# Constants in two loads, one more group of seven products, and new order tables in a one-core transformer step

## The chip, the cores and the metric

The kernel runs on one core of one Trainium2 chip. The metric is the device time of one execution in microseconds (us). TensorE is PE in the profile, VectorE is DVE, ScalarE is ACT, GpSimd is POOL, and SyncE, whose queue issues most of the DMAs, is SP. PEld is PE's loading of the stationary operand.

## What is computed

One layer for two groups of 128 tokens of width 2048, the context and the latent tokens. Cut to what matters:

```python
sh1, sc1, g1, sh2, sc2, g2 = silu(cond) @ w_ada + b_ada
h = rms_norm(x) * (1 + sc1) + sh1
qa, ka, va, qb, kb, vb, ga, gb = split(h @ w_in)       # q and k with RMS norms, rotary for A's latent tokens
o_a, o_b = attention_A(...), attention_B(...)           # A with a sink logit per head, B with a position bias
x = x + g1 * ((sigmoid(ga) * (o_a @ w_br_a) + sigmoid(gb) * (o_b @ w_br_b)) @ w_out)
h2 = rms_norm(x) * (1 + sc2) + sh2
x = x + g2 * (relu(h2 @ w_up) ** 2 @ w_down)
```

Outputs are both token groups and the context's new keys and values. All is float32.

## The kernel before

**Steps.** Every float32 operand is split into a high part that PE takes in one pass and the rest, and a product is three matmuls: high by high, low by high, high by low. The weights come as 456 steps. A plain step is one tile of 128x1024 (512 KB): SP loads it (`raw`), ACT copies its high part (`wH`, L112), DVE subtracts (`wL`, L272), and PE runs 12 matmuls of 512 columns (two row blocks, two token groups, three products; L347 to L349, at the start L474 to L476). `run()` goes through the steps in order, and the order on every engine comes from tables written into the file, mostly one digit for a step: `RUN` (how many steps ahead SP loads), `LOOK` and `AHEAD` (how many steps ahead DVE and ACT split), `DOTS` and `DOTS2` (at which steps DVE computes columns of the modulation, L1685), `JOBS` (at which steps the parts of the eight attention jobs run), `LO_DMA`, `XL_DMA`, `YL_DMA`, `T_DMA` (which subtractions POOL makes by a DMA that adds to its target, L278 and L279, in DVE's place).

**Groups of seven.** The up projection after its first two column blocks is done in pieces 1 to 7. A piece has eight positions of two steps each. A plain position takes 24 matmuls. A position named in `FAST` is a group of seven: it multiplies a two by two arrangement of blocks with seven products in place of eight, 21 matmuls, and ACT and DVE form sums of weight blocks for it (`t`, `XL`, `YB`, `tL`, `uL`; L1506 to L1517).

**Tiles.** Almost everything lies in one pool of `GEN` = 53 tiles of 128x1024 float32. A load waits until a tile is free. Some sums of the down projection (`DS_AWAY`) and two gates (`AWAY`) are written to memory and read back.

**Transposes.** An attention job transposes its probabilities either on PE, where it is named in `TE` (`probs_T`, L970), or in three parts: ACT writes the 16-bit halves apart (`probs_part`), SP issues a DMA transpose (`flip`, L1062), ACT joins the halves (`join_full`).

**Constants.** `load_consts` (L754) runs at step `CONST_AT[0]` and puts nine loads on SP's queue: the rope table, three norm weights and the sink logits, each of these four repeated over 128 partitions, and four caches. `pair_load` (L356) loads the tiles `araw` that PE uses as they are, for the first columns of the modulation (L365).

**Small tiles.** `SM` hands out small tiles from a ring of 14. `SCRATCH` is the size given to the program as `dynamic_dma_scratch_size`, which POOL's DMAs use.

Of the kernel before, what the change touches and what calls it, by code (L numbers as in the profile page):

```python
# [10 lines left out]
F32 = mybir.dt.float32  # L11
# [11 lines left out]
NH = 8  # L23
# [13 lines left out]
H_AT = 38  # L37
DOTS1 = [20, 27, 30, 34, 34, 34, 38, 42]
# [21 lines left out]
DIRECT = (3,)  # L60
LO_DMA = {186: 8, 205: 8, 218: 9, 357: 6, 402: 6, 448: 7, 455: 3}

LOOK = "320000020500002000113432224544355446105343223385524450433655335345220455511216541254444406744443240165443463136211143544456397555524342453545433224531546677753453557412434789853455586466303567898461134235331776545653214545433434534422123768733734502102522243854523655760005645555536452367642004332333245620031043144643220323340312252125324443413423321411333333446345833326123111223423654523544524557100124130023323212212653354124352222546524348984222137443"
RUN = "477775843203332344201115467652232043011000214655554545722223554564663425725104564635357113386532341025420431232200023641333255531301123352668485623663533674577742537976553665798745455424674845166864765894635788555673686472111145366178975888700000020012023644555422226413232347643568846245786634444454264413110226663556601331223412454545453312421521553234211233853234713364676798730111441302144857734435120022454125889556545654254345899778887778568999996432"
AHEAD = "431002222111211211100000000220000000000210121111110000000000011011122211000020133110000100000233000000011111112211133011020000023000000000000222001110010000000000000000111000222000100010221244331221020000000000011111000003022411110111110002000002111145220110000133444663455741000000000010001102100100000000000000000000000120000000000000112000211111223321000000000000000000000020000000000100000000011112223422222122100002120011100212112222234643010221345422"
CONST_AT = [73, 75]
XL_DMA = {9: 8, 16: 10, 21: 7, 23: 9, 26: 7, 35: 9, 38: 11, 43: 9, 55: 10, 61: 8}
ADA_G = ((1,), (2,), (3, 4), (5, 6))
ADA_AT = [None, 5, 14, 16, 22, 34, 40]
XS_AT = {1: 5, 2: 12, 3: 36}  # L70
POST = {('kvA', 0): [66, 70, 73], ('qA', 0): [66, 69, 75, 75, 77], ('qA', 1): [70, 75, 75, 82, 82], ('kB', 0): [75, 77, 79, 80, 82], ('qB', 0): [81, 82, 86, 88, 90], ('kB', 1): [84, 86, 91, 92, 95], ('qB', 1): [85, 92, 99, 100, 100]}
JOBS = [[80, 80, 81, 85, 88, 89, 92], [82, 83, 84, 86, 90, 97, 104], [83, 86, 86, 89, 90, 90, 105], [89, 91, 92, 93, 93, 105, 109], [95, 95, 98, 100, 100, 102, 114], [95, 101, 102, 104, 107, 111, 116], [106, 106, 108, 108, 121, 123, 127], [108, 111, 116, 117, 117, 120, 124]]
SS_G = [(0, 2), (2, 1)]
SS_AT = [53, 53, 73, 73, 125, 141]
T_AT = [3, 4]
PREP_IN = [4, 7]
DOTS = [37, 45, 46, 50, 50, 51, 52, 54, 56, 56, 56, 57, 61, 63, 65, 67, 70, 73, 77, 84, 89, 91, 92, 93, 96, 97, 102, 103, 104, 106, 108, 109, 109, 112, 114, 117, 118, 120, 122, 122, 123, 126, 129, 129, 129, 132, 133, 137, 138, 138, 140, 144, 145, 146, 156, 156, 156, 160, 160, 163, 167, 169, 173, 173, 175, 175, 178, 179, 179, 182, 182, 183]
DOTS2 = [225, 231, 234, 235, 237, 238, 245, 245, 258, 266, 268, 270, 270, 294, 300, 301, 306, 327, 328, 331, 333, 336, 349, 359, 360, 362, 363, 367, 394, 395, 396, 401]
# [12 lines left out]
def tile_hybrid_step(ctx: ExitStack, tc: tile.TileContext, a):  # L91
# [4 lines left out]
    sp = ctx.enter_context(tc.tile_pool(name="small", bufs=6))  # L96
# [3 lines left out]
    act, dve, pe, pool, sync = nc.scalar, nc.vector, nc.tensor, nc.gpsimd, nc.sync  # L100
# [37 lines left out]
    early = G("early")  # L138
# [615 lines left out]
    def load_consts():  # L754
        rope, wbg = G("rope"), cpadG[:, 640:1024]
        rc = rope[:, 0:256].rearrange("p (a b c) -> p a b c", a=2, b=4)
        sync.dma_start(rc.rearrange("p a b c -> p (a b c)"), a["rope"])
        wb = wbg.rearrange("p (a d) -> p a d", a=3)
        for n, name in enumerate(("q_norm_a", "k_norm_a", "k_norm_b")):
            sync.dma_start(wb[:, n, :], a[name][0].partition_broadcast(P))  # L760
        dve.tensor_scalar(wb, wb, float(HD) ** 0.5, None, op0=OP.mult)
        dve.tensor_scalar(qkw, qkw, float(HD) ** 0.5, None, op0=OP.mult)
        K2["wb"] = {"kvA": wb[:, 1, :], "kB": wb[:, 2, :]}

        for n, name in enumerate(("qA", "kvA")):
            t = rope[:, 256 * n + 256:256 * n + 512].rearrange("p (a b c) -> p a b c", a=2, b=4)
# [359 lines left out]
    for u in AWAY:  # L1126
        i = end_of(("y" + u[0][1].lower(), u[1]))
# [732 lines left out]
```

## Time and profile before

| what | before |
|---|---|
| median of 3 runs | 1313.22 us (1312.78 to 1313.6) |
| the profiled execution | 1312.65 us |
| its span, first to last instruction | 1310.8 us |
| PE busy in the span | 1303.2 us, 99% |
| DVE / ACT / POOL busy | 1126.5 / 904.5 / 57.4 us |
| mean granted clock of PE | 0.999 |

The profiled execution took 1.85 us more than its span; that lies outside the first and the last instruction. Busy PE includes the modelled ends of pipelined matmuls, so the pace is read from one start to the next.

### The profile page before, as it was taken

What the parts mean: (1) busy time and instruction counts of PE and PEld (TensorE: products, weight loads), DVE (VectorE), ACT (ScalarE), POOL (GpSimd) and SP (SyncE); (2) the same over time, 40 slices, a digit from 0 to 9 for tenths busy, and PEclk for the clock granted to TensorE, in tenths of its full rate; (3) what the DMA queues carried; (4) which work ended last, traced back from release to release, by engine and by line L of the source; (5) the groups of instructions that cost most, each with busy time, mean ns of one, the idle gap of its engine ahead of it and who ended that gap; (6) DMA issues with size and microseconds to landing.
All of it is one profiled execution on the core that took longest, in us unless ns stands there. A gap on an engine that the chain in (4) does not pass through costs nothing.

```text
span 1310.8 us, 17957 instructions
## 1 busy us (share of the span) xinstructions
PE 1303.2 (99%) x6333; PEld 1057.9 (81%) x6334; DVE 1126.5 (86%) x1446; ACT 904.5 (69%) x1145; POOL 57.4 (4%) x66
## 2 busy tenths in 40 slices
PE   9999999999999999999999999999999999999998
PEld 4778788788788878888888888888888888888887
DVE  4669799989999899999778998987999998789663
ACT  5635566699865655636786878859779597696980
POOL 0000000332000000000000000000000000000000
PEclk9999999999999999999999999999999999999999
DMA  9999999897999989997599789779977978869593
GB/s 371 408 409 408 400 409 389 346 321 232 271 347 349 386 294 365 359 334 235 205 300 318 204 269 287 275 269 273 322 240 238 362 245 278 301 205 367 193 355 96
DMA packets 170138, 400.90 MB, mean 306 GB/s; under 512 B 71840, under 2 KB 73088, under 8 KB 170048
## 3 DMA queue, kind: packets, MB, share of 16 engines
q1 hardware_dynamic: 165744, 387.36, 82.3%
q0 software_dynamic: 4160, 12.32, 5.0%
q8 instruction: 49, 0.80, 0.2%
q14 instruction: 41, 0.34, 0.1%
q10 hardware_dynamic: 144, 0.08, 0.1%
HBM read 373.97 MB, written 10.80 MB: 294 GB/s over the span
## 4 chain that ended last, share of the span: by engine, by line
PE 98%; ACT 1%; DMA 1%; SPq 0%; issue 0%; DVE 0%; ACTq 0%
PE acc L347 17%; PE acc L348 17%; PE acc L349 17%; PE Q L1421 6%; PE Q L1420 6%; PE Q L1419 6%; PE acc L474 5%; PE acc L475 5%; PE acc L476 5%; PE ps_ada L365 3%; PE ps_S L920 1%; PE Z L1421 1%; PE Z L1420 1%; PE Z L1419 1%; DMA araw<-in_w_pair 1%; PE acc L1225 1%
## 5 line engine op out<-in xcount | busy, mean ns | idle before, releaser
L272 DVE TENSOR_TENSOR wL<-raw,wH 128x1024 fp32r<-128x1024 f32 x377 | 442.7, 1219 | 51.2 <-ACT wH L112 49.0
L112 ACT ACTIVATE wH<-raw 128x1024 fp32r<-128x1024 f32 (+1 forms) x394 | 388.5, 1039 | 62.3 <-DMA raw<-in_w_in 22.6
L474 PE MATMUL acc<-wH,hH 128*128 128x512 f32 x272 | 107.1, 394 | 0.6 <-ACT srow L112 0.6
L475 PE MATMUL acc<-wL,hH 128*128 128x512 f32 x272 | 105.9, 389 | 0.0
L476 PE MATMUL acc<-wH,hL 128*128 128x512 f32 x272 | 105.9, 389 | 0.0
L347 PE MATMUL acc<-wH,hH 128*128 128x512 f32 x252 | 101.2, 402 | 0.0
L348 PE MATMUL acc<-wL,hH 128*128 128x512 f32 x252 | 98.3, 390 | 0.0
L349 PE MATMUL acc<-wH,hL 128*128 128x512 f32 x252 | 98.2, 390 | 0.0
L1685 DVE CUSTOM_DVE_ANT_0 aT<-aT,cB,cols 128x1024 f32<-128x1024 f32 x56 | 71.4, 1283 | 0.6
L1685 DVE CUSTOM_DVE_ANT_0 junk<-aT,cB,cols 128x1024 bf16<-128x1024 f32 x56 | 71.2, 1279 | 0.0
L112 ACT ACTIVATE uH<-raw 128x1024 fp32r<-128x1024 f32 x34 | 36.1, 1062 | 47.4 <-DVE raw L1514 38.2
L474 PEld LDWEIGHTS acc<-wH,hH 128*128 128x128 f32 x272 | 51.0, 188 | 14.2 <-issue 2.9
L476 PEld LDWEIGHTS acc<-wH,hL 128*128 128x128 f32 x272 | 51.1, 188 | 10.8
L475 PEld LDWEIGHTS acc<-wL,hH 128*128 128x128 f32 x272 | 51.1, 188 | 10.2
L347 PEld LDWEIGHTS acc<-wH,hH 128*128 128x128 f32 x252 | 47.4, 188 | 10.6 <-issue 1.0
L348 PEld LDWEIGHTS acc<-wL,hH 128*128 128x128 f32 x252 | 47.4, 188 | 10.5 <-issue 0.7
L349 PEld LDWEIGHTS acc<-wH,hL 128*128 128x128 f32 x252 | 47.3, 188 | 9.9
L112 ACT ACTIVATE tH<-t 128x1024 fp32r<-128x1024 f32 x31 | 32.8, 1058 | 30.4 <-DVE t L1506 26.2
L112 ACT ACTIVATE fTa<-pTa 128x2048 uint16<-128x2048 uint16 x16 | 40.5, 2533 | 1.3 <-DVE gc_g L1685 1.3
L1685 DVE CUSTOM_DVE_ANT_0 aT<-aT,cB,gc_g 128x1024 f32<-128x1024 f32 x32 | 40.7, 1282 | 0.4
L1685 DVE CUSTOM_DVE_ANT_0 junk<-aT,cB,gc_g 128x1024 bf16<-128x1024 f32 x32 | 40.7, 1280 | 0.0
L1562 ACT ACTIVATE up<-up 128x1024 f32<-128x1024 f32 x28 | 29.7, 1062 | 15.4 <-DVE up L1552 14.9
(694 smaller groups left out, 3351.9 us busy)
## 6 DMA issues: line engine op xcount, KB each, us to landing
raw<-in_w_in SPq DMA_DIRECT2D x131, 512.0 KB, 9.0
raw<-in_w_down SPq DMA_DIRECT2D x128, 512.0 KB, 6.8
araw<-in_w_pair SPq DMA_DIRECT2D x80, 512.0 KB, 9.8
raw<-in_w_upF SPq DMA_DIRECT2D x68, 512.0 KB, 6.3
aT<-in_w_gT SPq DMA_DIRECT2D x64, 512.0 KB, 7.1
raw<-in_w_up SPq DMA_DIRECT2D x60, 512.0 KB, 6.8
aT<-in_w_adaT SPq DMA_DIRECT2D x48, 512.0 KB, 8.0
raw<-in_w_out SPq DMA_DIRECT2D x32, 512.0 KB, 7.8
```

Source lines behind the costliest of these rows:

```text
L112: act.activation(out, in_, AF.Copy)
L272: dve.tensor_tensor(st["lo"], st["raw"], st["hi"].bitcast(F32), op=OP.subtract)
L347: pe.matmul(acc[tb], sh, wh[:, k, :], start=f, stop=False, **kw)
L348: pe.matmul(acc[tb], sh, wl[:, k, :], start=False, stop=False, **kw)
L349: pe.matmul(acc[tb], sl, wh[:, k, :], start=False, stop=l, **kw)
L474: pe.matmul(acc[tb], sh, wh[:, k, :], start=kt == 0 and k == 0 and not held and not seeded, stop=False, **kw)
L475: pe.matmul(acc[tb], sh, wl[:, k, :], start=False, stop=False, **kw)
L476: pe.matmul(acc[tb], sl, wh[:, k, :], start=False, stop=last and k == 1 and not hold, **kw)
L1419: pe.matmul(acc, stat[0], hi, start=f, stop=False)
L1420: pe.matmul(acc, stat[0], lo, start=False, stop=False)
L1421: pe.matmul(acc, stat[1], hi, start=False, stop=l)
L1685: dve.tensor_tensor_reduce(out, box["raw"], cB[s, tag], 1.0, dst if second else baT[:, part, fb:fb + 1], OP.mult, OP.add, dst)
```

## The change

- The rope table, the sink logits and the three norm weights stand in one array of 128 rows; two loads read it. The two small sink tiles are made from the loaded row by DVE.
- `FAST` names 35 positions, before 34. Piece 3 has six groups (positions 0 to 2 and 5 to 7), and piece 7 has three in a row (2 to 4).
- `GEN` is 54. `SCRATCH` is 1024 in place of 4096, small tiles are 16 wide in place of 32 and their ring is 12, which makes room. `sg` lies in the tile `early`.
- The job of mixer A, context tokens, second head group leaves `TE`: its probabilities are transposed by DMA.
- All tables of the order are new.

```diff
-GEN = 53
-SCRATCH = 4096
+GEN = 54
+SCRATCH = 1024
-TE = (('A', 0, 1), ('qA', 1), ('qB', 1))
-DS_AWAY = [8, 9, 12, 15, 19, 21, 22, 23]
+TE = (('qA', 1), ('qB', 1))
+DS_AWAY = [0, 13, 14, 19, 21, 22]
-FAST = {1: (0, 1, 5, 7), 2: (0, 2, 3, 5, 7), 3: (0, 2, 3, 5, 7), 4: (0, 1, 3, 6, 7), 5: (0, 1, 3, 5, 7), 6: (0, 1, 3, 5, 7), 7: (0, 1, 3, 5, 7)}
+FAST = {1: (0, 1, 3, 7), 2: (0, 2, 3, 5, 7), 3: (0, 1, 2, 5, 6, 7), 4: (0, 1, 3, 4, 7), 5: (0, 1, 3, 4, 7), 6: (0, 1, 3, 5, 7), 7: (0, 2, 3, 4, 7)}
-LO_DMA = {186: 8, 205: 8, 218: 9, 357: 6, 402: 6, 448: 7, 455: 3}
+LO_DMA = {200: 7, 258: 3, 285: 8, 320: 7, 347: 5, 350: 5, 383: 9, 439: 5, 452: 10, 454: 5}
...
     def SM(n, name):
-        return sp.tile([P, 32], F32, name=name, tag="s", bufs=14)[:, :n]
+        return sp.tile([P, 16], F32, name=name, tag="s", bufs=12)[:, :n]
...
-    sg = SM(32, "sg")
+    sg = early[:, 672:704]
...
-        sync.dma_start(rc.rearrange("p a b c -> p (a b c)"), a["rope"])
+        sync.dma_start(rope[:, 0:256 + NH], a["consts"][:, 0:256 + NH])
         wb = wbg.rearrange("p (a d) -> p a d", a=3)
-        for n, name in enumerate(("q_norm_a", "k_norm_a", "k_norm_b")):
-            sync.dma_start(wb[:, n, :], a[name][0].partition_broadcast(P))
+        sync.dma_start(wbg, a["consts"][:, 256 + NH:])
...
-        sync.dma_start(sk[:, 0, :], a["sink_a"][0].partition_broadcast(P))
-        dve.tensor_scalar(sk[:, 1, :], sk[:, 0, :], -1.0, None, op0=OP.mult)
+        for i in range(2):
+            dve.tensor_scalar(sk[:, i, :], rope[:, 256:256 + NH], 1.0 - 2 * i, None, op0=OP.mult)
...
+    rows = np.concatenate([x[n].reshape(-1) for n in ("sink_a", "q_norm_a", "k_norm_a", "k_norm_b")])
+    out["consts"] = np.concatenate([_rope_table(), np.broadcast_to(rows, (P, rows.size))], 1)
```

The order of PE before, at the one place where the job that leaves `TE` transposed its probabilities (between steps of the gates; `ps_PT` is the PSUM bank, `prob` the probabilities):

```order
L347 MATMUL acc<-wH,hH_840 128x512
L348 MATMUL acc<-wL,hH_840 128x512
L349 MATMUL acc<-wH,hL_841 128x512
L970 MATMUL ps_PT<-ident,prob 128x128 x4
L347 MATMUL acc<-wH,hH_840 128x512
L348 MATMUL acc<-wL,hH_840 128x512
```

In the changed program no row of PE names `ps_PT`. SP's queue of the changed program has the transpose of that job instead, as the fourth of these rows (`pTPA` and `plPA` are its halves, `pTqB` and `pTkB` belong to other tiles):

```order
L1061 DMA_TRANSPOSE pTqB_3016<-plqB_3013 128x16x128
L1061 DMA_TRANSPOSE pTPA_3027<-plPA_2982 128x8x128
L1061 DMA_TRANSPOSE pTPA_3154<-plPA_3029 128x16x128
L1061 DMA_TRANSPOSE pTPA_3156<-plPA_3109 128x8x128
L243 DMA raw<-in_w_in 128x1024
L1672 DMA aT<-in_w_adaT 128x1024
```

Before, three transposes stood there, and the same loads behind them. DVE's order in piece 7, before, around its second group:

```order
L1516 TENSOR_TENSOR tL<-t_10716,tH 128x1024
L1517 TENSOR_TENSOR uL<-raw,uH 128x1024
L272 TENSOR_TENSOR wL<-raw,wH 128x1024 x2
L1506 TENSOR_TENSOR t_10815<-raw 128x1024
L1510 TENSOR_TENSOR XL<-raw,XH 128x1024
```

And in the changed program, through the second of the three groups that follow each other:

```order
L1515 TENSOR_TENSOR tL<-t_10744,tH 128x1024
L1516 TENSOR_TENSOR uL<-raw,uH 128x1024
L1505 TENSOR_TENSOR t_10775<-raw 128x1024
L1509 TENSOR_TENSOR XL<-raw,XH 128x1024
L1510 TENSOR_TENSOR raw<-t_10775,raw 128x512
L1512 TENSOR_TENSOR YB<-raw,YB 128x512
L1513 TENSOR_TENSOR raw<-raw 128x512
L1515 TENSOR_TENSOR tL<-t_10775,tH 128x1024
L1516 TENSOR_TENSOR uL<-raw,uH 128x1024
L1505 TENSOR_TENSOR t_10861<-raw 128x1024
```

Before, the two subtractions of a plain position stood behind every second group at the latest; now three groups follow each other without them.

## Rows read from the trace of the kernel before

**Rows 1.** The page: busy time by engine, and PE's granted clock in 40 slices
```profile
PE 1303.2 (99%) x6333; PEld 1057.9 (81%) x6334; DVE 1126.5 (86%) x1446; ACT 904.5 (69%) x1145; POOL 57.4 (4%) x66
...
PEclk9999999999999999999999999999999999999999
```
**Rows 2.** PE's waits, longest in total first: us in total, times, longest
```profile
PE ps_warm L136 <- DVE wm L129: 1.2, 1, 1.2
PE ps_ss L171 <- ACT sq L168: 0.8, 1, 0.8
PE acc L474 <- ACT srow L112: 0.6, 1, 0.6
```
**Rows 3.** Windows: stretch, its length, busy us by engine, PEclk, DMA share, GB/s
```profile
0.00:36.00 36.00, 32.42 (x189) 16.40 (x190) 17.59 (x41) 20.50 (x39) 2.07 (x10) 1.00 0.97 374
36.00:270.00 234.00, 233.95 (x1420) 183.49 (x1421) 197.78 (x288) 136.37 (x195) 19.24 (x20) 1.00 1.00 390
270.00:480.00 210.00, 210.00 (x1046) 172.76 (x1045) 193.93 (x275) 152.41 (x233) 10.47 (x9) 1.00 0.93 323
480.00:620.00 140.00, 140.00 (x624) 115.92 (x623) 136.93 (x176) 78.69 (x86) 2.95 (x3) 1.00 0.90 317
700.00:1300.00 600.00, 600.00 (x2649) 496.71 (x2649) 511.08 (x572) 453.61 (x511) 17.36 (x20) 1.00 0.82 272
```
**Rows 4.** PE's timeline in piece 7, second group: first matmul, first use of uL
```profile
1184.12 0.39 PE L1419 MATMUL Q<-XH,h20H 128*128 128x512 f32 x1
...
1187.75 0.39 PE L1420 MATMUL Q<-uL,h20H 128*128 128x512 f32 x1
```
**Rows 5.** PE's timeline around the transposes of probabilities: start us, us, what
```profile
309.90 0.60 PE L970 MATMUL ps_PT<-ident,prob 128*128 128x128 f32 x4
310.25 0.48 PE L347 MATMUL acc<-wH,hH 128*128 128x512 f32 x1
310.57 0.40 PE L348 MATMUL acc<-wL,hH 128*128 128x512 f32 x1
```
**Rows 6.** Timelines of SP and ACT around the transposes by DMA
```profile
302.31 12.55 SPq L1062 DMA_TRANSPOSE pTPA<-plPA  x2
314.95 1.08 SPq L243 DMA_DIRECT2D raw<-in_w_in  x1
...
317.78 0.58 ACT L112 ACTIVATE PT<-ps_PT 128x512 f32<-128x512 f32 x1
```
**Rows 7.** DMA issues of the constants: count, KB each, median us to landing
```profile
rope<-in_rope SPq DMA_DIRECT2D x1, 128.0 KB, 5.0
...
cpad<-in_k_norm_b SPq DMA_DIRECT2D x1, 64.0 KB, 6.8
```
**Rows 8.** DVE's timeline in piece 7, first and second group
```profile
1173.73 1.22 DVE L1506 TENSOR_TENSOR t<-raw 128x1024 f32<-128x1024 f32 x1
...
1176.60 0.69 DVE L1513 TENSOR_TENSOR YB<-raw,YB 128x512 fp32r<-128x512 f32 x1
...
1180.29 1.22 DVE L1506 TENSOR_TENSOR t<-raw 128x1024 f32<-128x1024 f32 x1
...
1185.76 1.23 DVE L1517 TENSOR_TENSOR uL<-raw,uH 128x1024 fp32r<-128x1024 f32 x1
1186.90 2.35 DVE L272 TENSOR_TENSOR wL<-raw,wH 128x1024 fp32r<-128x1024 f32 x2
```
**Rows 9.** The tiles araw in 140 to 158 us: PE, SP's issues, landing
```profile
L365 PE MATMUL ps_ada<-araw,cpad x64: 379/379/405, 154.7 to 158.0; 128*32 128x256 f32 x64
L356 SPq DMA_DIRECT2D araw<-in_w_pair x8: 328/350/384, 141.2 to 146.8; - x8
...
DMA to landing us min/median/max: 4.0/6.0/7.4
```
**Rows 10.** POOL: one issue in its timeline, and the page's group of these DMAs
```profile
659.70 0.89 POOL L279 DMA_DIRECT2D XL<-in_w_upF  x1 [23.99 <-DVE sfull L1403]
...
XL<-in_w_upF POOLq DMA_DIRECT2D x10, 512.0 KB, 7.3
```

More of the change, by code (lines that the diff above doesn't have):

```diff
@@ L36 @@
 FB1 = 14
-H_AT = 38
-DOTS1 = [20, 27, 30, 34, 34, 34, 38, 42]
+H_AT = 22
+DOTS1 = [19, 31, 31, 33, 37, 38, 38, 42]
 CHUNKS = [2, 2, 2, 4, 6]
@@ L44 @@
 EXTRA = (('gB', 0),)
-TE = (('A', 0, 1), ('qA', 1), ('qB', 1))
-DS_AWAY = [8, 9, 12, 15, 19, 21, 22, 23]
+TE = (('qA', 1), ('qB', 1))
+DS_AWAY = [0, 13, 14, 19, 21, 22]
 DS_BACK = 6
-YL_DMA = [8, 9, 15, 23, 29, 31, 39]
-T_DMA = {15: 10, 48: 10, 55: 7}
+YL_DMA = [15, 16, 24, 29, 31, 39, 48, 63]
+T_DMA = {11: 10, 15: 10, 20: 9, 55: 7}
 G2_PARTS = 1
-PREP_LATE = 9
-G2_LEAD = 2
-ADA_LD = [1, 1, 0, 2, 0, 0, 0]
+PREP_LATE = 4
+G2_LEAD = 1
+ADA_LD = [0, 1, 3, 2, 0, 1, 0]
 BEGIN_SEED = ()
-FAST = {1: (0, 1, 5, 7), 2: (0, 2, 3, 5, 7), 3: (0, 2, 3, 5, 7), 4: (0, 1, 3, 6, 7), 5: (0, 1, 3, 5, 7), 6: (0, 1, 3, 5, 7), 7: (0, 1, 3, 5, 7)}
@@ L56 @@
-AWAY = [('gB', 0), ('gB', 3)]
-GATE_BACK = 3
-SEED_IN = {3: -1, 4: -1}
+FAST = {1: (0, 1, 3, 7), 2: (0, 2, 3, 5, 7), 3: (0, 1, 2, 5, 6, 7), 4: (0, 1, 3, 4, 7), 5: (0, 1, 3, 4, 7), 6: (0, 1, 3, 5, 7), 7: (0, 2, 3, 4, 7)}
+AWAY = [('gB', 2), ('gB', 3)]
+GATE_BACK = 1
+SEED_IN = {3: -1, 4: 0}
 SEED_AT = 4
 DIRECT = (3,)
-LO_DMA = {186: 8, 205: 8, 218: 9, 357: 6, 402: 6, 448: 7, 455: 3}
-LOOK = "320000020500002000113432224544355446105343223385524450433655335345220455511216541254444406744443240165443463136211143544456397555524342453545433224531546677753453557412434789853455586466303567898461134235331776545653214545433434534422123768733734502102522243854523655760005645555536452367642004332333245620031043144643220323340312252125324443413423321411333333446345833326123111223423654523544524557100124130023323212212653354124352222546524348984222137443"
@@ new lines @@
+RUN = "600000002166845278641126577763452132555334515644874458823334543454772335725104453635367113364223451125420420433311133742321044430122323330027386836885744775587553769799888888587767677623574857168965861997535788977796898582112255366289975888700001010012023643455422226424343468543578947354663412222454243314331337773545600572333412455543453532410521542123100025964345712253576843200012774524355847945557341022443004889557677876353112577979787756303445885310"
+AHEAD = "200000000000000000010000000000000222000000022102010000001211100020010210000010133110222322220223100121133222233322333200003255466465000000000000011111030000011000000012111002333200000000341244020100020000000002320000000003023411000133332223001226552456553430002025333551455741000000000011000003100000002220000000000000000120000000000000001000200111123363222222011000201121111131112211124422222200011112223422222123000202100001100200013121123545251212345424"
@@ L68 @@
+CONST_AT = [73, 63]
+XL_DMA = {9: 7, 16: 8, 19: 5, 21: 8, 23: 9, 31: 7, 32: 10, 38: 10, 39: 8, 43: 9, 44: 6, 55: 9, 61: 10, 62: 9}
 ADA_G = ((1,), (2,), (3, 4), (5, 6))
[L69 to L72, printed above, removed]
+ADA_AT = [None, 5, 14, 20, 24, 31, 40]
@@ new lines @@
+XS_AT = {1: 11, 2: 16, 3: 42}
+POST = {('kvA', 0): [58, 70, 73], ('qA', 0): [62, 70, 75, 75, 77], ('qA', 1): [67, 75, 75, 81, 82], ('kB', 0): [76, 77, 78, 79, 82], ('qB', 0): [77, 82, 86, 86, 90], ('kB', 1): [84, 89, 91, 93, 102], ('qB', 1): [86, 96, 96, 96, 98]}
+JOBS = [[80, 80, 83, 85, 86, 89, 93], [81, 81, 84, 86, 90, 94, 105], [83, 86, 87, 89, 90, 90, 105], [89, 90, 92, 93, 93, 107, 111], [94, 96, 101, 105, 105, 107, 119], [96, 103, 105, 106, 111, 112, 117], [104, 107, 108, 108, 119, 123, 128], [106, 112, 113, 118, 118, 119, 123]]
@@ L73 @@
 SS_G = [(0, 2), (2, 1)]
[L74 removed]
+SS_AT = [52, 73, 70, 73, 140, 140]
 T_AT = [3, 4]
[L76 to L78 removed]
@@ L79 @@
-STAT_AT = [2, -1, 9, 1]
-T_PAIR = [[14, 4], [6, 9], [8, 8], [5, 8], [8, 9], [5, 10], [6, 12]]
-P_PAIR = [[5, -1], [1, 1], [0, 5], [1, 5], [1, 6], [0, 5], [3, 0]]
+PREP_IN = [5, 7]
+DOTS = [35, 46, 50, 50, 50, 52, 54, 54, 56, 56, 56, 56, 57, 62, 64, 67, 70, 73, 77, 84, 89, 91, 92, 93, 96, 97, 102, 103, 104, 106, 108, 109, 109, 112, 114, 117, 118, 120, 122, 122, 123, 126, 127, 128, 129, 130, 135, 138, 138, 138, 140, 144, 145, 148, 155, 156, 157, 160, 161, 163, 167, 169, 172, 173, 173, 175, 178, 179, 179, 181, 183, 189]
@@ L82 @@
+DOTS2 = [227, 231, 234, 234, 237, 238, 245, 245, 264, 264, 265, 267, 270, 290, 300, 302, 304, 327, 331, 333, 333, 334, 349, 359, 360, 362, 365, 367, 392, 395, 396, 400]
+STAT_AT = [4, 2, 10, 12]
+T_PAIR = [[14, 7], [6, 6], [7, 9], [9, 9], [9, 10], [9, 9], [11, 12]]
+P_PAIR = [[4, -1], [2, 2], [1, 3], [3, 5], [-1, 2], [3, 3], [-1, 3]]
 M_TE = (3,)
-M_AT = [1, 2, 6]
+M_AT = [1, 2, 8]
 FLIP = 1
-P_UP = [4, 2]
-T_UP = [13, 11]
+P_UP = [5, 3]
+T_UP = [13, 13]
 COL = {"qA": 0, "kvA": 1024, "qB": 1536, "kB": 2560, "vB": 3584, "gA": 4608, "gB": 6656}
@@ L765, in load_consts @@
         for n, name in enumerate(("qA", "kvA")):
-            t = rope[:, 256 * n + 256:256 * n + 512].rearrange("p (a b c) -> p a b c", a=2, b=4)
+            t = rope[:, 256 * n + 256 + NH:256 * n + 512 + NH].rearrange("p (a b c) -> p a b c", a=2, b=4)
             w4 = wb[:, n, :].rearrange("p (b c) -> p b c", c=32)
@@ L1804, in tiles @@
         return w.reshape(k // 256, 2, P, m // n, n).transpose(0, 3, 2, 1, 4).reshape(k // 256, m // n, P, 2 * n)
-    out = {n: x[n] for n in ("x_prompt", "x_sample", "b_ada", "q_norm_a", "k_norm_a", "q_norm_b", "k_norm_b", "sink_a",
-                             "cache_a_v", "cache_b_v")}
+    out = {n: x[n] for n in ("x_prompt", "x_sample", "b_ada", "cache_a_v", "cache_b_v")}
     for n in ("w_in", "w_br_a", "w_br_b", "w_out", "w_up", "w_down"):
@@ L1849 @@
     given = _layout({n: np.asarray(inputs[n]) for n in _INS})
-    given["rope"] = _rope_table()
     for n, v in given.items():
```

5 lines of the change are left out of this document (1 added, 4 removed).

## The prediction, made before the changed kernel was run

> **What bounds the kernel now.** I read the page first. [...] Busy time of PE has modelled ends in it, so I read PE's waits next: the whole span has five, 3.3 us together, and the last one ends at 36.05 us [rows 2]. Then the windows: PE is idle 3.6 us in the first 36 us, and in every stretch from 36 to 1300 us it is busy throughout, while DVE has 16 to 36 us to spare in the stretches up to 480 us, 3.1 us in 480 to 620, and 89 us behind 700 [rows 3]. The timelines give the pace. In piece 7 sixteen matmuls start between 1184.12 and 1187.75 us, 0.227 us each [rows 4]. So the time is a start of 36 us, then the number of PE's matmuls times their pace, then a short end. The other engines and the queue count only where they become late.
>
> **The start and the end.** By the order of the changed program all engines run the same instructions up to the first plain step near 36 us, apart from the place of one small tile. PE's and DVE's last rows, from the last unit's sums on, are also the same. Both: 0 us.
>
> **PE's work.** One group of seven more takes 21 matmuls in place of 24: 3 times 0.227 is 0.68 us less. The job that leaves `TE` takes four transposes from PE. They start at 309.90; the wide matmul behind them starts at 310.25, and the next at 310.57 [rows 5]. Without them that second matmul would start 0.227 after 309.90, so the block costs 0.67 - 0.23 = 0.44 us, a slower first matmul behind it included. By the order PE has 5942 matmuls before and 5935 after, and all kinds but these are equal. Sum of PE's own work: 1.12 us less. Since PE waits for nothing, all of it lies on the path.
>
> **The transposes by DMA.** ACT gains two copies and a join and loses one copy of 0.58 us [rows 6], about 2 us in a stretch where it is idle 57 of 210 us [rows 3]. SP's queue gains one transpose ahead of four weight loads. There the queue stood 12.55 us on two such transposes, because one of them waited for a free tile, and the loads went out at 314.95 [rows 6] without PE waiting. Below: 0, if one tile more ends that wait earlier. Above: half of 12.55, 6.3 us, if nothing hides it. I take 0, since the nearer row is that of the 12.55 us, which PE did not feel.
>
> **Constants.** Three loads fewer. The rope load took 5.0 us to land and a norm weight up to 6.8 [rows 7]; SP's loads go on behind them, and nothing of PE's waits there. A gain of three short issues on SP has no place to show: 0 us. If it moved the queue by a whole landing, 6.8 us, it would still only make loads earlier that PE does not wait for.
>
> **Tiles, away sums, small tiles.** Two sums fewer travel to memory and back, in a stretch where the DMA share is 0.82 [rows 3]: 0 us, covered by the spare DMA time. The small ring of 12 can only hold up a softmax, by one job's DVE or ACT instruction, and DVE has 16 us to spare there: 0 us. The subtraction of one step of the out projection returns from POOL to DVE: 1.2 us, half of the pair at 1186.90 [rows 8], against 3.1 us of spare in 480 to 620 us. It fits; if that spare is gone, PE waits 1.2 us.
>
> **Three groups of seven in a row.** This is the tightest place that I find. DVE starts the groups of piece 7 at 1173.73 and 1180.29: 6.56 us a group [rows 8], and PE takes 21 x 0.227 = 4.77. Each group costs DVE 1.79 us of its lead. A plain position takes DVE 2.35 us and PE 24 x 0.227 = 5.45, which gives back 3.1. Before, no more than two groups stand together, and after two DVE ends `uL` at 1186.99 [rows 8] for a use at 1187.75 [rows 4]: 0.76 us of lead are left. So one group leaves 2.55. In the new piece 7 the sequence is group, plain, three groups: 2.55 + 3.1 - 5.37 = 0.3 us left, no wait. In the new piece 3 it starts with three groups: 2.55 - 3.58 = -1.03, and POOL makes the subtraction for `YB` at the first of them, 0.69 us [rows 8]: PE waits 0.34 us if that piece is entered as piece 7 was. The third run stands behind two plain positions and fits. Below 0, above 1.8 us for each of the three runs; I take 0.3 us in all.
>
> **Sum.** 1.12 less and 0.3 more: 0.8 us less, in a profiled execution of 1312.65 us with a span of 1310.8. The median of the runs shown is 0.57 us above it, so I forecast 1313.22 - 0.8 = 1312.4 us.
>
> **The rivals.**
>
> *DVE bounds the runs of three (slower).* The leads above hold if DVE enters each run with as much stock as the old piece 7 had. Against a run without stock, PE waits 3 x 1.79 = 5.4 us, in three runs 16 us. It decides from 3.7 us of waits in all, which take back 1.1 and go 2.6 beyond: some 1.25 us of stock missing beyond the sums above at each of the three. With 2 us missing at each the time is 1313.2 - 1.1 + 6 + 0.3 = 1318. For it: DVE is busy 511 of 600 us behind 700 [rows 3], the leads are below 1 us, and the tables that place its other work are all new. Against it: the spare is 89 us, and PE waited for nothing at leads this small. Chance 0.11.
>
> *Early tiles of the modulation come late (same).* Up to 270 us the DMA share is 1.00 [rows 3], so every tile placed ahead of another costs it 512 KB at 390 GB/s, 1.3 us. The group of eight `araw` at 154.7 us issues its last tile at 146.8 and lands it 7.4 us later, 154.2, half a microsecond before PE begins [rows 9]; the last of the eight is used 3 us later. Counted through SP's order, that group's last tile is the 116th in both programs and PE has the same work ahead of it. The later groups are as well placed or better, but for the last of this stretch, one tile later. If that and a second such place don't fit, and the out projection's subtraction shows too, PE waits 1 to 3 us: 1313 to 1315.5, about 1314. Chance 0.17.
>
> *POOL's DMAs run out of room (slower).* An issue on POOL takes 0.89 us and the transfer lands 7.3 us later [rows 10]; the order has four output transfers in a row near 250 us. If POOL had to wait there for landings, the norms queued behind them would be late by up to 3 x 7.3 - 3 x 0.89, 19 us. A quarter of this reaching PE gives about 1317. [...] Chance 0.03.
>
> *The new order merges small blocks of PE (faster).* The slow first matmul behind a block costs about 0.1 us (0.32 against 0.227, [rows 5]). Fifteen blocks merged would add 1.5 us to the 1.1 and give 1310.5. The order shows blocks moved, not that many merged. Chance 0.05.
>
> **How the numbers follow.** The forecast itself, waits below 1 us in all, has 0.64. A measurement of this kernel can tell about 0.2%, 2.6 us, from no change. Faster by more is the last rival: 0.05. Slower by more is DVE's runs and POOL's room: 0.14. Within: 0.64 + 0.17 = 0.81. The range leaves out the faster rival and the slower ones: 1310.8 to 1316.0.
>
> **What would show it.** Right: PE's list of waits stays as it is, PE's span is about 1 us shorter, the row with `ps_PT` is gone and the group count is 35. `uL` in the runs of three ends less than 1 us ahead of its use. Wrong: PE waits for `uL`, `tL` or `wL` by DVE in pieces 3 or 7, for `araw` before 260 us, or for tiles behind the fourth transpose; a clock below full in a stretch would be outside all of this.

## The result, and the profile after

| | before | changed |
|---|---|---|
| median | 1313.05 us (6 runs, 1312.56 to 1313.6) | 1318.31 us (6 runs, 1316.66 to 1320.47) |
| ratio, 95% interval | | 1.004 (1.0029 to 1.005) |
| span of the profiled execution | 1310.8 us | 1315.6 us |

The change makes the kernel slower by 5 us, 0.4%. Forecast were 1312.4 us and a range from 1310.8 to 1316.0, so both are wrong. The page of the changed kernel reads as that of before [rows 1]:

```profile
PE 1303.3 (99%) x6326; PEld 1056.3 (80%) x6327; DVE 1132.7 (86%) x1452; ACT 911.1 (69%) x1151; POOL 61.0 (5%) x66
...
PEclk9999999999999999999999999999999999999999
```

What differs is PE's list of waits. It had five, 3.3 us, the last of which ended at 36.05 us [rows 2]. Now it has nine; the first eight are (us in total, times, longest):

```profile
PE acc L475 <- DVE wL L272: 2.5, 1, 2.5
PE ps_ss L171 <- ACT sq L168: 1.6, 1, 1.6
PE ps_warm L136 <- DVE wm L129: 1.2, 1, 1.2
PE acc L1240 <- DVE wL L272: 1.0, 2, 0.7
PE acc L474 <- ACT srow L112: 0.6, 1, 0.6
PE ps_sel L383 <- ACT S L112: 0.5, 1, 0.5
PE ps_ada L365 <- DMA araw<-in_w_pair: 0.3, 1, 0.3
PE Q L1418 <- ACT dsum L112: 0.3, 1, 0.3
```

The windows say where (length, busy us of PE, PEld, DVE, ACT, POOL, granted clock, DMA share, GB/s):

```profile
36.00:270.00 234.00, 231.09 (x1406) 180.63 (x1407) 196.60 (x288) 132.38 (x193) 21.92 (x19) 1.00 1.00 389
270.00:480.00 210.00, 210.00 (x1045) 173.08 (x1044) 193.89 (x273) 154.64 (x233) 12.24 (x10) 1.00 0.91 319
480.00:620.00 140.00, 138.96 (x616) 114.39 (x616) 136.60 (x175) 80.01 (x86) 0.95 (x1) 1.00 0.91 325
700.00:1300.00 600.00, 599.70 (x2644) 495.26 (x2643) 512.84 (x572) 464.14 (x522) 19.19 (x22) 1.00 0.82 271
```

Against [rows 3], PE is busy 2.9 us less from 36 to 270, 1.0 less from 480 to 620 and 0.3 less behind 700. DVE's own work is hardly more in any stretch; it is late at single places. PE's timeline there (start us, us, what, in brackets the idle time ahead and what ended it):

```profile
247.95 0.50 PE L475 MATMUL acc<-wL,hH 128*128 128x512 f32 x1 [2.46 <-DVE wL L272]
...
614.02 0.50 PE L1240 MATMUL acc<-wL,m2H 128*128 128x512 f32 x1 [0.37 <-DVE wL L272]
...
617.70 0.50 PE L1240 MATMUL acc<-wL,m3H 128*128 128x512 f32 x1 [0.67 <-DVE wL L272]
```

Counted from one matmul's start to the next, beyond the pace of 0.227, PE loses 2.7 us at 247.95, 0.5 at 614.0, 0.8 at 617.7, 0.2 at 722, 0.2 at 851 and 0.5 at 1102: 4.9. With 0.4 at the start, and less the 1.1 us of work that left PE as forecast, that is 4.2 of the 4.8 us between the spans. The rest lies in gaps of 0.1 us that I did not follow one by one; a slower matmul right behind each stall is among them (0.334 from start to start behind the one at 247.95).

**The largest place.** SP's timeline ahead of the constants, first in the kernel before, then in the changed one:

```profile
225.25 0.33 SPq L243 DMA_DIRECT2D raw<-in_w_in  x1
225.67 0.38 SPq L1673 DMA_DIRECT2D aT<-in_w_adaT  x1
226.14 2.38 SPq L243 DMA_DIRECT2D raw<-in_w_in  x2
228.62 0.37 SPq L757 DMA_DIRECT2D rope<-in_rope  x1
```

```profile
224.68 2.06 SPq L356 DMA_DIRECT2D araw<-in_w_pair  x4
226.83 0.75 SPq L243 DMA_DIRECT2D raw<-in_w_in  x1
227.67 1.02 SPq L1672 DMA_DIRECT2D aT<-in_w_adaT  x1
228.78 1.08 SPq L243 DMA_DIRECT2D raw<-in_w_in  x2
230.25 0.33 SPq L757 DMA_DIRECT2D rope<-in_consts  x1
231.95 0.33 SPq L759 DMA_DIRECT2D cpad<-in_consts  x1
```

In the changed kernel eight tiles of 512 KB, 4 MB, are issued in the 5.6 us ahead of the first load; by an estimate from the 389 GB/s of the stretch they take 10.8 us to move. Before the change four tiles were issued in as long a time. The issues of 225 to 250 us (KB each, us to landing) show how long the two loads take now, where [rows 7] had 5.0 and 6.8 us:

```profile
cpad<-in_consts SPq DMA_DIRECT2D x1, 192.0 KB, 9.6
rope<-in_consts SPq DMA_DIRECT2D x1, 132.0 KB, 10.8
```

DVE's timeline shows who feels it. The first row is the first use of the constants in the kernel before, which had no idle time ahead; the others are of the changed kernel:

```profile
238.10 0.35 DVE L761 TENSOR_SCALAR cpad<-cpad 128x384 f32<-128x384 f32 x1
```

```profile
238.16 0.08 DVE L1684 DVE_READ_ACCUMULATOR2_ANT gc_g<- 128x1 f32 x1
241.59 0.36 DVE L760 TENSOR_SCALAR cpad<-cpad 128x384 f32<-128x384 f32 x1 [3.35 <-DMA cpad<-in_consts]
...
246.68 2.43 DVE L272 TENSOR_TENSOR wL<-raw,wH 128x1024 fp32r<-128x1024 f32 x2
```

DVE takes its work in the order of the program, as these rows show: it stands (sits idle with later work behind it) for 3.35 us at its first use of the constants, and the subtraction that PE wants at 245.2 ends behind that, at 247.9. The product that needs the scaled weights comes only at 253.3.

Seven profiles, of kernels that load the constants in this place, show the same chain at different lengths. The kernels are those of the experiments below.

| kernel | last row that DVE needs landed at | DVE stood | PE waited for `wL` |
|---|---|---|---|
| join at 6 steps | 239.1 | 1.1 | 0.3 |
| piece 3 old | 240.4 | 1.7 | 0.8 |
| changed, second profile | 240.9 | 3.0 | 2.1 |
| subtraction by the load | 241.4 | 3.2 | 2.3 |
| changed, first profile | 241.6 | 3.4 | 2.5 |
| 53 tiles | 242.7 | 4.2 | 3.5 |
| five loads | 243.1 | 5.2 | 4.5 |

PE's wait is DVE's stand less 0.7 to 0.9 us in every row. The first five rows are of kernels that differ in nothing that bears on the constants, so the size of this loss changes from one execution to the next.

### The profile page after: what moved, and what is told of

Its sections match the earlier page's. It is cut to its first block, busy times and chain, and to the rows that moved or that the text cites. A ratio compares the mean times of both kernels' runs of the same rounds, so it can differ in the third digit from the quotient of the medians.

```text
span 1315.6 us, 17965 instructions
## 1 busy us (share of the span) xinstructions
PE 1303.3 (99%) x6326; PEld 1056.3 (80%) x6327; DVE 1132.7 (86%) x1452; ACT 911.1 (69%) x1151; POOL 61.0 (5%) x66
## 4 chain that ended last, share of the span: by engine, by line
PE 89%; DVE 4%; DMA 3%; ACT 2%; issue 1%; SPq 0%; DVEq 0%; ACTq 0%
PE acc L347 16%; PE acc L348 16%; PE acc L349 16%; PE Q L1418 6%; PE Q L1419 6%; PE Q L1420 6%; PE acc L474 4%; PE acc L475 4%; PE acc L476 4%; PE ps_ada L365 2%; DMA araw<-in_w_pair 2%; DVE wL L272 2%; PE ps_S L919 1%; DVE aT L1684 1%; DMA cpad<-in_consts 1%
## 5 line engine op out<-in xcount | busy, mean ns | idle before, releaser
L112 ACT ACTIVATE dsum<-acc 128x512 f32<-128x512 f32 x56 | 31.2, 589 | 15.1 <-PE acc L349 14.2
```

The lines of the kernel that those rows point to most:

```text
L112: act.activation(out, in_, AF.Copy)
```

## The experiments

All times below are medians against the kernel before on the same chip (1313.3 to 1313.5 us), with the ratio and its interval. Two groups do most of the work: parts of the change alone in the kernel before, and single places mended in the changed kernel. Where a length of a wait is given from one matmul's start to the next, beyond the pace, it is 0.1 to 0.3 us longer than in PE's list. Theory Q is the reading above: what stands ahead of the constants on SP's queue sets when they land, and DVE's stand for them makes PE wait.

### Parts of the change, alone in the kernel before

Two loads in place of five:

> The kernel before with its constants as two loads instead of five, nothing else changed (tables, 53 tiles, small tiles as before). Theory Q: the two loads land near 237 us as the five did, no wait of TensorE appears between 230 and 260 us, and the time is within 0.1 per cent of the kernel before (1312 to 1314.5). Rival T (the form of the two loads is slow by itself): they land after 240 us, VectorE stands for them, TensorE waits for over 1 us near 245, and the time is 1314.5 to 1316.

Measured 1313.35 us, 0.9999 (0.999 to 1.0008). The loads land at 234.2 and 235.2 us, and PE waits for nothing there. Theory Q.

54 tiles, with the smaller small tiles and scratch, and the two loads of the run above:

```diff
-GEN = 53
-SCRATCH = 4096
+GEN = 54
+SCRATCH = 1024
...
```

> The kernel before with the room made and filled alone: constants in two loads, smaller small tiles, the smaller scratch of the accumulating loads, 54 large tiles; all order tables as before. Theory O (the time was lost to the order alone): no wait of TensorE after 40 us over 0.5 us, constants landing before 240 us, 1312.3 to 1314.3 us. Rival E (one more large tile lets 512 KB more in ahead of the constants, and the smaller scratch holds up the accumulating loads): constants after 240 us with a TensorE wait of over 1 us at 245 to 250, or waits for accumulated tiles after 700 us; 1314.5 us or more.

Measured 1313.62 us, 1.0001 (0.9993 to 1.001), no new wait after the start, constants at 233.6 and 234.0. Theory O.

Three groups of seven in a row:

```diff
-3: (0, 2, 3, 5, 7)
+3: (0, 1, 2, 5, 6, 7)
```

> The kernel before with one thing changed: piece 3 has its groups of seven at positions (0, 1, 2, 5, 6, 7) instead of (0, 2, 3, 5, 7), six instead of five, with two runs of three. Theory R: three matmuls fewer, 0.7 us gained, and one wait for ScalarE's copy of down sums in the first run of three, 0.2 to 1.2 us at 845 to 852 us, none or under 0.3 us in the second run; so between 0.5 us under and 0.5 us over the kernel before (1312.8 to 1313.8). Rival V (VectorE's subtraction itself is late in each run of three, up to 1.8 us each): TensorE waits for low parts by VectorE in both runs, over 2 us together, and the time is 1314.5 or more. Rival G (nothing waits): 1312.6.

Measured 1312.85 us, 0.9995 (0.9986 to 1.0004). One new wait, 0.5 us for ScalarE's copy of a down sum at 846.8, none in the second run: theory R, with 0.6 of the 0.7 us given back in the profile.

The fourth transpose by DMA (one step of the same job in `JOBS` moves from 86 to 87 with it):

```diff
-TE = (('A', 0, 1), ('qA', 1), ('qB', 1))
+TE = (('qA', 1), ('qB', 1))
```

> The kernel before with one thing changed: the job of the third group of mix A has its transposes done by the DMA like the others, not by TensorE (its part, flip and join at the steps that the change gives them). Theory N (the transposes fit beside the weight loads, as forecast): four small transposes leave TensorE, 0.4 us gained, no wait of TensorE over 0.4 us between 280 and 340 us, 1312.6 to 1313.4. Rival L (the queue of weight loads stands for the transposes' tile or behind them, up to 6.3 us): a wait of TensorE for a weight tile or for ScalarE or VectorE behind it between 300 and 340 us, over 1 us, and 1314.2 or more.

Measured 1313.39 us, 1.0 (0.9991 to 1.0009). In the profile PE waits once behind the start, for a `wL` at 336 us; the 0.4 us lost there are what the four transposes gained. Theory N, at its edge.

The late join and the subtraction on DVE together:

```diff
-M_AT = [1, 2, 6]
+M_AT = [1, 2, 8]
-LO_DMA = {186: 8, 205: 8, 218: 9, 357: 6, 402: 6, 448: 7, 455: 3}
+LO_DMA = {205: 8, 218: 9, 357: 6, 402: 6, 448: 7, 455: 3}
```

> The kernel before with only the two edits that are held to cause the waits at 612 to 618 us: the join of a mixed tile at 8 steps instead of 6, and the subtraction of piece 186 on VectorE instead of by the accumulating load. Theory J (the late join stands VectorE for about 1.9 us, and that with 1.2 us for the subtraction uses up 3.1 us of spare): VectorE stands for ScalarE's high part near 545 us for over 1 us, TensorE waits 0.3 to 1.5 us between 605 and 622 us, and the time rises by as much, to 1313.6 to 1314.8. Rival I (the old order has room for both): no wait over 0.2 us there, 1313.3 within 0.5.

Measured 1313.51 us, 1.0001 (0.9993 to 1.001), PE waits for nothing there, DVE never stands over 0.5 us between 530 and 610. Rival I: the old order has room for both, and theory J falls as a full cause.

So none of the parts tried costs anything by itself, within intervals of 0.1%. Not tried alone were the new groups of pieces 1, 4, 5 and 7, the sums and gates sent to memory, and the other tables. What is left is the order written by the tables, and the parts together in it.

### The changed kernel again, and with single places mended

> The changed kernel itself, for a second profile and as the measure of the three kernels beside it. If the stalls are stalls of order (VectorE and ScalarE each held at the head of a strict queue), the same places show again: 245 to 250 us, 612 to 618, 850 and 1101; how long each lasts may differ, since the landing of the constants was 241.6 us in the first profile and 239.1 us in the kernel with the early join (its wait at 248 then 0.5 us instead of 2.7). Time 1316.5 to 1320. If the waits lie in other places, they are disturbances of single executions.

Measured 1318.44 us, 1.0043 (1.003 to 1.0055). The same places: 2.4 us at 247, 0.6 and 0.8 at 615 and 619, 0.2 at 724 and 852; at 1101 nothing.

The use of the constants later on DVE:

```diff
     load_at(CONST_AT[0], load_consts)
+    at(69, use_consts)
```

> The changed kernel with one thing moved: the nine small VectorE operations that use the constants come after four more pieces of VectorE work (two dot products, a sum, two weight subtractions, some 7 us), the two loads stay where they are on the load queue. Theory Q (the constants' loads stand behind about 4 MB of tiles, land at 241.6 us, and VectorE, which takes its work in strict order, stands 3.35 us at its first use of them while the subtraction that TensorE needs at 247.9 waits behind): TensorE's wait of 2.5 us at 248 is gone, the loads still land near 241 to 242, and the time falls by 2 to 3 us, to about 1315.5. Rival D (VectorE is simply too full before 248 us, whatever it waits for): a wait of over 1.5 us stays at 248 and the time stays within 1 us of 1318.3.

Measured 1318.16 us, 1.0031 (1.002 to 1.0043). The loads land at 240.3 and 240.8, and the wait at 248 is gone, as theory Q says. The time did not follow, though a fall of 2 to 3 us was expected: in the profile 0.5 us came at 289 and 1.1 at 850. The profiled execution took 1316.0 us, the second quickest of six, so the median holds losses that the profile does not show.

The loads earlier on SP's queue, DVE's use left in its place:

```diff
-    load_at(CONST_AT[0], load_consts)
+    load_at(69, load_consts)
+    load_at(CONST_AT[0], use_consts)
```

> The changed kernel with the two loads of the constants issued nine tiles earlier on the load queue, ahead of the four tiles of w_pair; VectorE's use of them stays where it is. Theory Q (what stands ahead of them on the queue sets their landing): they land before 236 us, VectorE does not stand for them, TensorE's wait at 246 to 249 us (2.7, 2.4, 2.6, 1.1 and 0.5 us in five profiles) is gone, and the time is 1.5 to 2.7 us under the changed kernel's 1318.4, about 1316 to 1317. Rival O (the order of VectorE's work alone, full to that place): the loads land early, but over 1 us of the wait stays.

Measured 1316.31 us, 1.0024 (1.0015 to 1.0032). The issues of 215 to 240 us of this kernel, and DVE's timeline at the same instruction as above:

```profile
cpad<-in_consts SPq DMA_DIRECT2D x1, 192.0 KB, 6.3
rope<-in_consts SPq DMA_DIRECT2D x1, 132.0 KB, 6.4
```

```profile
237.82 0.07 DVE L1689 DVE_READ_ACCUMULATOR2_ANT gc_g<- 128x1 f32 x1
237.82 0.35 DVE L764 TENSOR_SCALAR cpad<-cpad 128x384 f32<-128x384 f32 x1
```

They land at 227 us, DVE goes through without a stand, and PE's wait is gone: theory Q, 2.1 us by the medians. The two intervals still overlap a little (up to 1.0032 here, from 1.003 there); the eleven executions took 1313.71 to 1317.53 us, eleven of the changed kernel 1316.66 to 1320.79.

Five loads in the changed order (the old `load_consts`, all tables kept):

> The changed kernel with the constants loaded by five loads again, as before the change, in the same place, all tables and 54 tiles kept. Theory Q (what stands ahead of them on the load queue sets when they land, not their number or form): the last of the three weight rows lands between 241 and 245 us, VectorE's stand of 3 us or more and TensorE's wait of over 2 us at 248 stay, and the time is between 1317 and 1321. Rival T (two loads of 132 and 192 KB take longer to land than five smaller ones): the weight rows land by 239 us, the wait at 248 is under 1 us, and the time is about 1315.5.

Measured 1323.07 us, 1.007 (1.0057 to 1.0084). The last weight row lands at 243.1 and DVE stands 5.2 us. The first row of PE's list:

```profile
PE acc L475 <- DVE wL L272: 4.5, 1, 4.5
```

Rival T is excluded. The time is beyond theory Q's 1321; in its profile the lower clock came with the longer wait, 0.50 from 249 to 252 us (last section). So by the medians the two loads are worth 4.7 us here and nothing in the old order.

53 tiles in the changed order:

```diff
-GEN = 54
+GEN = 53
```

> The changed kernel with 53 large tiles instead of 54, all else kept. If the 54th tile is what puts more tiles ahead of the constants, they land a micro-second or more earlier (about 239.5) and the wait at 248 shrinks below 1.5 us, with the time near 1317. If the order of the tables does it, they land at 240 to 242 again and the wait stays over 2 us. If the changed order lives on the 54th tile, waits for weight tiles (data from the loads, not from VectorE) appear after 40 us, and the time is 1319.5 or more; if none of these, 1318.4 within 0.7.

Measured 1321.36 us, 1.0065 (1.0052 to 1.0077). The constants land at 242.2 and 242.7, so the order puts them late, not the 54th tile. PE waits 3.5 us for the `wL` behind them. New waits: 1.0 us for a `wL` at 451, two of 0.3 at 368 and 726, and 0.2 for a loaded `YB`. By the medians the changed order lives on its 54th tile, for 3 us; the old one gains nothing from it.

The join at 6 steps:

```diff
-M_AT = [1, 2, 8]
+M_AT = [1, 2, 6]
```

> The changed kernel with the join of a mixed tile (copy, high part, low part) at 6 steps after its last product instead of 8, as before the change. Theory J (at 8 steps the join's high part reaches ScalarE only at 549.5 us, VectorE stands 1.9 us for it at 550.6, and its lead is used up by 614 us): TensorE's two waits at 614 and 617.7 us, 1.4 us together, fall below 0.3, and the time falls by about 1.2 us, to about 1317. Rival S (the weight subtraction that came back from the load engine, 1.2 us, uses the lead up by itself): at least 0.8 us of the two waits stay, and the time stays within 0.5 us of 1318.3.

Measured 1317.54 us, 1.0033 (1.002 to 1.0045). The wait at 614 is gone, 0.8 us at 616 stays, and 0.8 is new at 549, where PE now waits for the next mixed tile `g_gA`. Neither theory J nor rival S holds in full. The profiled execution also waited 1.1 us at 850, and only 0.3 us at 245 behind the constants, so its 1316.4 us don't tell what the join is worth. What prompted the run is this row of the changed kernel, against none before:

```profile
550.64 1.22 DVE L116 TENSOR_TENSOR m2L<-fTm,m2H 128x1024 fp32r<-128x1024 f32 x1 [1.91 <-ACT m2H L112]
```

The subtraction back on the load:

```diff
-LO_DMA = {200: 7, 258: 3, ...}
+LO_DMA = {186: 8, 200: 7, 258: 3, ...}
```

> The changed kernel with one weight subtraction of w_out (piece 186) given back to the accumulating load, as before the change; VectorE has one subtraction of 1.22 us less ahead of 612 us. Theory S (what is missing at 614 and 617.7 us is VectorE's time: 1.9 us lost at the late join plus 1.2 us for the subtraction against the 3.1 us that were spare): the two waits, 1.4 us, fall to 0.3 or less, the time by about 1.2 us. Rival W (VectorE's spare there is set at its last stand after 550 us by what ScalarE or the loads deliver): over 0.8 us of the waits stay.

Measured 1317.43 us, 1.0035 (1.0021 to 1.0048). The first wait goes, 0.7 us of the second stays: between theory S and rival W. The profile of this kernel also shows best what happens in a run of three groups (DVE, ACT and PE in order of time):

```profile
849.15 0.69 DVE L1513 TENSOR_TENSOR raw<-raw 128x512 f32<-128x512 f32 x1
...
849.94 1.06 ACT L112 ACTIVATE uH<-raw 128x1024 fp32r<-128x1024 f32 x1 [2.00 <-DVE raw L1513]
...
850.90 1.06 ACT L112 ACTIVATE dsum<-acc 128x512 f32<-128x512 f32 x2
...
851.54 0.50 PE L1418 MATMUL Q<-tH,sH 128*128 128x512 f32 x1 [0.85 <-ACT dsum L112]
```

ACT stands 2.0 us for DVE's sum of the next group, and behind it in ACT's order are the two copies that free the accumulators which PE wants. ACT takes its work in the order of the program, as DVE did above, so a late DVE reaches PE through ACT, long before its own result is due.

Piece 3 on its old positions:

```diff
-3: (0, 1, 2, 5, 6, 7)
+3: (0, 2, 3, 5, 7)
```

> The changed kernel with piece 3 on its old five positions with groups of seven, (0, 2, 3, 5, 7), so without three in a row at its start; 34 groups in all. Theory R (in a run of three, VectorE falls behind TensorE, ScalarE stands for VectorE's data ahead of the copies that free TensorE's accumulators, and TensorE waits for those copies at 850 us: 0.2 us in one profile, 1.1 and 1.2 in two others): no wait for such a copy between 840 and 860 us; against the changed kernel beside it, plus 0.7 us of matmuls and minus 0.2 to 1.2 us of waits, so within 1 us of it. Rival P (ScalarE is late there for another reason, e.g. the order of the down products before it): a wait of at least 0.5 us for the copy stays between 840 and 860 us, and the time is about 0.7 us above the changed kernel's.

Measured 1318.57 us, 1.0037 (1.0024 to 1.0049). No wait for such a copy is left: theory R. The time is within 1 us of the changed kernel's, as expected.

Three at once (constants used later, subtraction by the load, piece 3 old):

> The changed kernel with three things mended at once: the use of the constants later, the w_out subtraction by the load, piece 3 on its old positions. If the time was lost at the places seen (2.7 at 248 us, 1.4 at 612 to 618, 0.2 to 1.2 at 850), these waits are gone, 0.2 us at 720 and 0 to 0.5 us at 1101 stay, and the four transposes by TensorE that left (0.4 us) are gained: 1313 to 1314 us, no slower than the kernel before by more than 0.1 per cent, and its runs spread by less than 2 us instead of 4. If it stays above 1315.5, something else that runs through the whole program (the 54 tiles, the loads' order) costs time.

Measured 1315.17 us, 1.0016 (1.0007 to 1.0025), spread 2.3 us. Three of the five microseconds are back. One by one the three edits gave 1.2 us, but those medians are of five or six executions that spread over 2.5 to 4 us, so whether the edits help each other is not shown. The profiled execution, the quickest of eleven, shows 0.3 us at 289, 0.6 at 364, 0.3 at 615 and 0.2 at 719. Two of these mended too:

```diff
-JOBS = [[80, ...], [81, ...], ..., [94, ...], ...]
+JOBS = [[80, ...], [82, ...], ..., [95, ...], ...]
```

> The kernel with three things mended (1315.2) and two steps more: the score products that waited at 289 us for a transposed tile by ScalarE (0.3 us) and at 364 us for an accumulator that VectorE had not yet copied out (0.6 us) come one step later, at 82 and 95 as before the change. If the rest of the loss is such places too, both waits go and the time falls by about 0.9 us to 1314.3, within 0.2 per cent of the kernel before. If the waits come back at other places, the time stays at 1315.2 within 0.4: then the changed order as a whole has less spare than the old one, and mending single places does not help.

Measured 1315.62 us, 1.0017 (1.0008 to 1.0026). The wait at 289 is gone, 0.5 at 364 stays, 0.8 at 615 and 0.3 at 1099 are back. The second expectation, 1315.2 within 0.4, holds at its edge: moving these two steps did not help.

### More groups of seven, for a kernel faster than both

```diff
+FAST = {1: (0, 1, 5, 7), 2: (0, 1, 3, 4, 6, 7), 3: (0, 1, 3, 4, 6, 7), ... the same up to 7}
```

> The kernel before with six groups of seven in each of pieces 2 to 7, always at positions (0, 1, 3, 4, 6, 7), so in pairs only; 40 groups instead of 34, all other tables as before. If VectorE's spare in a piece (about 13 us of 82) can be used wherever the groups stand, 18 matmuls of 0.227 us leave the path: minus 4.1 us, 1309.2. Rival K (a run of groups is paid out of the lead built just before it, and what six groups take, 4.5 us more than in a piece of five, is not rebuilt in time): TensorE waits for ScalarE's copies or for low parts by VectorE in most of the six pieces, 0.5 to 1.5 us in each, and the time is 1311 to 1316.

Measured 1333.71 us, 1.0158 (1.0144 to 1.0171). PE's list, first rows:

```profile
PE Q L1419 <- ACT dsum L112: 6.5, 2, 3.7
PE Q L1419 <- ACT uH L112: 2.6, 2, 1.8
PE acc L347 <- ACT acc L112: 2.2, 3, 1.4
PE Q L1420 <- DVE uL L1517: 1.9, 3, 0.8
```

```diff
+FAST = {1: (0, 1, 5, 7), 2: (0, 2, 3, 5, 6, 7), 3: (0, 2, 3, 5, 6, 7), 4: (0, 1, 3, 4, 6, 7), 5: (0, 1, 3, 4, 5, 7), 6: (0, 1, 3, 5, 6, 7), 7: (0, 1, 3, 5, 6, 7)}
```

> The kernel before with one group of seven added in each of pieces 2 to 7 beside the five that stand there (position 6 in pieces 2, 3, 6 and 7, position 4 in pieces 4 and 5), so that each accumulating load keeps its group; 40 groups. Without waits minus 4.1 us, 1309.2. With waits as in the kernel with piece 3 alone changed (0.6 us for one copy) in each piece: minus 0.5, 1312.8. Rival K (the lead isn't rebuilt from piece to piece): waits grow from piece to piece, over 4 us in all, and the time is 1313.5 or more.

Measured 1326.58 us, 1.0098 (1.0085 to 1.0112):

```profile
PE acc L347 <- ACT acc L112: 4.2, 5, 1.8
PE Q L1419 <- ACT uH L112: 1.3, 2, 1.0
PE acc L348 <- DVE wL L272: 1.2, 2, 0.8
```

Rival K, and worse than it said in the first kernel, where the granted clock also fell, to 0.96 from 760 to 843 us, a stretch in which PE was idle 3.8 us. Six groups more save 4.1 us of matmuls, and the time rises by 13 and 20. DVE's idle time in a piece, 5 to 18 us in windows of 83 to 85 us of the kernel before, does not stand where the added groups need it, not with these tables. No version faster than both came out.

## Why the prediction was wrong

**PE is the bound, and its work falls by 1.1 us: right.** PE is still busy wherever it does not wait, `ps_PT` is gone, and 7 matmuls fewer run. The traces count 6333 and 6326; the prediction's 5942 and 5935 stand in no trace, but their difference is right.

**Constants, "SP's loads go on behind them, and nothing of PE's waits there": this step failed, for the largest amount.** It took the landing of 5.0 to 6.8 us from the queue of before, and did not read the new order of SP, where eight tiles stand ahead of the two loads instead of four. It also looked at who waits for the constants' product and not at what stands behind their first use on DVE, and its bound of a whole landing only asked what earlier loads would gain, not what a later landing would cost. Measured: 9.6 to 10.8 us to landing, a stand of 3.35, 2.7 us of PE; with the loads moved ahead of the tiles the wait is gone and the median 2.1 us lower.

**The subtraction of the out projection, "1.2 us against 3.1 us of spare; it fits": failed as a sum.** PE lost 1.4 us at 614 to 618, in waits of 0.4 and 0.7. The 3.1 us were the idle time of the old order. The changed order leaves DVE 3.4 us in that stretch, but spends 1.9 of them in one stand for the late join. Yet the same two edits in the old order cost nothing, so these two are not the whole cause; what else of the new tables lies there stays open.

**Three groups in a row, 0.3 us: the size came out by luck, the mechanism was wrong.** The rate at which DVE falls behind was right. In piece 3 `uL` of the second and third group ends here, and PE uses it there:

```profile
850.32 1.23 DVE L1516 TENSOR_TENSOR uL<-raw,uH 128x1024 fp32r<-128x1024 f32 x1
856.94 1.23 DVE L1516 TENSOR_TENSOR uL<-raw,uH 128x1024 fp32r<-128x1024 f32 x1
```

```profile
857.99 0.39 PE L1419 MATMUL Q<-uL,h20H 128*128 128x512 f32 x1
...
862.75 0.39 PE L1419 MATMUL Q<-uL,h21H 128*128 128x512 f32 x1
```

The lead falls from 6.4 to 4.6 us, 1.8 a group as forecast [rows 8]; in the run of piece 7 it falls from 6.5 over 4.7 to 2.8. But the stock at entry was not that of the old piece 7: forecast were leads of 0.3 there and below 0 here. So the sign "less than 1 us ahead of its use" did not come, and PE does not wait for `uL`. It waits for ACT's copies in piece 3, 0.2 us in the first profile and 0.2 to 1.2 in others.

**The transposes (0), the tiles (0), the room of POOL's DMAs: no cost seen.** The fourth transpose alone moves nothing, nor do the tiles and small tiles; the sums sent to memory were not tried alone. That POOL might have to wait for landings near 250 us was a supposition. The changed kernel never has more than three of POOL's transfers between issue and landing (those issued at 250.57, 254.06 and 254.61 us landed 6.0, 6.0 and 6.2 us later), and POOL stood there only for data of ACT and DVE, 1.14, 2.69 and 1.72 us ahead of three of the four issues. What happens with more of them at once no run here shows.

**The rivals.** None named the constants. That of the early tiles had the out projection's subtraction among its waits of 1 to 3 us, and this one came; its tiles `araw` did not make PE wait behind 36 us. The one that ends near the measured time, DVE as the bound of runs of three at 1318, is wrong in place: it would have shown waits for `uL` in pieces 3 and 7. What came is the sum of several places that had been covered, most of them priced at zero because PE had not felt them under the old order. The sign "a clock below full in a stretch" came in the second profile, 0.54 from 249 to 252 us (last section).

**What stays open.** After the mended places some 2 us remain, and the single executions of the changed order differ by 4 us (1316.66 to 1320.79), those of the old by 2. A part of this seems to go with the clock: of the changed kernel's eleven executions the five with a mean granted clock of 1.000 took 1316.7 to 1318.4 us, and the six at 0.998 or 0.999 took 1318.4 to 1320.8. That is a hint, not a proof, since 0.999 occurs in executions of the old kernel too. It is not all of it, as the eleven with the loads ahead have 1.000 throughout and differ by 3.8 us. The profiled execution of the kernel with the loads ahead took 1313.71 us, the quickest of eleven with a median of 1316.31: what the slower ten lost, and where, no profile here shows.

## What to carry to other kernels

When a change comes with new order tables, do not take over from the old order that a delay is covered: for each load that is first used by an engine that takes its work in the order of the program, as DVE did here (it stood 3.35 us for the constants with later work behind it), read in the new order what stands ahead of it on its queue and what stands behind its first use. A part that costs nothing alone can still cost in the new order; here none of the parts tried cost anything alone, and the whole change costs 5 us. Issue a small load early rather than just in time: nine tiles earlier, the two loads here brought no new wait into PE's list, and their late landing was the largest single loss.

## What the runs showed of the hardware

The granted clock fell after a short wait of PE, and not always. In the second profile of the changed kernel PE waited 2.1 us at 247, and the clock stood at 0.54 behind it (window, length, busy us, granted clock, DMA share, GB/s):

```profile
246.50:249.00 2.50, 1.72 (x6) 0.87 1.04 415
249.00:252.00 3.00, 3.00 (x9) 0.54 1.03 410
252.00:256.00 4.00, 4.00 (x19) 1.00 1.03 413
```

In the first profile the wait was longer, 2.5 us, and the clock stayed at 1.00 (with 53 tiles, where the wait was 3.5 us, the mean granted clock of the profiled execution was 1.000):

```profile
249.00:252.00 3.00, 3.00 (x15) 1.00 1.03 410
```

Nine matmuls ran in those 3 us instead of 15, six fewer, so by an estimate at 0.227 each the fall cost about 1.4 us on top of the wait. With five loads, where the wait was 4.5 us, the clock stood at 0.64 from 246.5 to 249, 0.50 from 249 to 252 and 0.74 from 252 to 256. Here such a stall cost more than half as much again in one execution and nothing more in another. What decides whether the clock falls behind a wait no run here shows.
